# Seven block products in all fourteen inner tiles of a conv-GLU, with sums and a low part made by adding transfers

## The chip, the core and the metric

The kernel runs on one core of a Trainium2 chip. Its time is device microseconds of one execution of the program; the number compared is the median over runs. The engines are named as in the profile: PE multiplies matrices, PEld is its loading of weights, DVE (VectorE) and ACT (ScalarE) work element by element, POOL (GpSimd) and SP (SyncE) here issue transfers. Every engine takes its instructions in order, and they meet through semaphores.

## The reference, cut to what matters

The program computes two layers of an encoder trunk over 512 frames of width 1024: a time-mixing layer and a chunk-attention layer, each followed by the channel mixer that the change concerns. With D_FF = 2816:

```
def conv_glu(h, w_in, conv_w, conv_b, w_out):
    gate, val = jnp.split(h @ w_in, 2, axis=-1)             # (512, 1024) @ (1024, 2 * 2816)
    gp = jnp.pad(gate, ((0, 0), (2, 0), (0, 0)))
    conv = conv_b + sum(conv_w[j] * gp[:, j:j + 512] for j in range(3))
    return (jax.nn.gelu(conv) * val) @ w_out

x = x + conv_glu(rms_norm(x, ln2[layer]), ffn_in[layer], ffn_conv[layer], ffn_conv_b[layer], ffn_out[layer])
```

## The kernel before

All activations lie transposed, 128 channels on the partitions and 512 frames along a row. A product in full precision is made of three in the type float32r: a number is split into a high part (a rounding cast, on ACT) and a low part (what the rounding left, a subtraction on DVE), and high times high, high times low and low times high are summed in PSUM. `split_w` (lines 168 to 179) does it for weights: line 172 casts `whi`, and then either line 178 subtracts on DVE to give `wlo`, or, where a source in DRAM is given, line 175 writes the negated high part with ACT and line 176 lets POOL issue a transfer that adds the weights out of DRAM onto it. Before the change the second way is used in the first mixing layer and in part of an output projection alone. `wraw` has two buffers, `whi` and `wlo` have three each, handed out in turn to whoever splits weights next.

A channel mixer (`ffn`) makes 22 hidden tiles of 128 channels, j = 0 to 21, each from a gate tile and a value tile of weights (128 x 1024 floats, 512 KB each), and then an output stage. There are two kinds of hidden tile.

`eight(j)` multiplies plainly: for the gate and for the value 8 blocks of weights, three matmuls of 512 columns each, 48 matmuls in all (lines 201, 202 and 206, in `dense`).

`seven(j)` treats the gate and the value weights as a 2 x 2 matrix of halves, against two halves of the frames, and gets along with seven block products instead of eight (`prod`, lines 416, 417 and 419; each has 12 matmuls of 256 columns: eight with `whi`, alternating over the high and the low part of the activations, then four with `wlo`). Four of the products use sums of the activations that are made once per mixer (`sums`, tiles `xh` and parts of `f3h`, `f3l`); the others use the activations as they are. On the side of the weights each tile needs four sums or differences of halves (512 columns each), and the splits of all operands: `wv` (the value weights as loaded), `w1`, `w2`, `wx` and `w4`. Lines 435 and 439 to 441 make the sums on DVE. PSUM tiles `b` and `c` take up several products one after the other, and are read out (lines 447, 451, 456, 457, 461, 463) between one and the next. `gated(j, ...)` then applies convolution, gelu and gate (lines 389 to 393) and splits the hidden tile (lines 218 and 219).

Before the change the tiles 4, 5, 7, 8, 10, 11, 13, 14, 16 and 17 are sevens: ten of 22 in each of the two mixers, in pairs with an eight between them. The list is `SEVEN`. The loop in `ffn` runs the first product of a tile, then the last two products of the tile before it, then the tile's own middle. What is written there is not quite the order on the engines: a scheduler puts the instructions of DVE, ACT, POOL and SP in an order of its own, within the dependences. PE keeps to the program. A tile buffer that is handed out again makes its new writer wait for the last reader of the old content; on SP and POOL, where transfers are issued in order, everything behind a waiting issue waits too.

Of the kernel before, what the change touches and what calls it, by code (L numbers as in the profile page):

```python
# [13 lines left out]
ALU = mybir.AluOpType  # L14
# [98 lines left out]
def trunk_kernel(ctx, tc, A, out):  # L113
    nc = tc.nc
    PE, V, SC, GP = nc.tensor, nc.vector, nc.scalar, nc.gpsimd
# [28 lines left out]
    def ps_d(shape=(P, S)):  # L144
        return banks["D"].tile(list(shape), F32, name="psd", tag="psd")
# [7 lines left out]
    def ps_f(shape=(P, S)):  # L153
        return banks["F"].tile(list(shape), F32, name="psf", tag="psf")
# [8 lines left out]
    def tmp(dt=F32, shape=(P, S)):  # L163
        return banks["tmp"].tile(list(shape), dt, name="tmp", tag="tmp")
# [4 lines left out]
    def split_w(raw, n, src=None):  # L169
        hi = wp.tile([P, 1024], F32R, name="whi", tag="whi")  # L170
        lo = wp.tile([P, 1024], F32R, name="wlo", tag="wlo")
        SC.copy(hi[:, :n], raw)  # L172
        if src is not None:

            SC.activation(lo[:, :n], raw, AF.Copy, scale=-1.0)
            GP.dma_start(lo[:, :n], src, accum_op=ALU.add)
        else:
            V.tensor_tensor(lo[:, :n], raw, hi[:, :n], op=ALU.subtract)  # L178
        return hi, lo
# [37 lines left out]
    def split_to(h_, l_, src):  # L217
        SC.copy(h_, src)
        V.tensor_tensor(l_, src, h_, op=ALU.subtract)  # L219
# [124 lines left out]
            V.tensor_tensor(xT[:, m], xT[:, m], ps[:], op=ALU.add)  # L344
            norm_tile(xT[:, m], m, gain, h_, l_)

    SEVEN = [j for j in range(4, 18) if j % 3 != 0]
    HT = (slice(0, 256), slice(256, 512))

    def ffn(l, hp, ih, il, h_, l_, xT, after, last=None):  # L350
# [8 lines left out]
        def low(k):  # L359
            return (f3h, f3l)[k // 2][:, 10 + 2 * (k % 2):12 + 2 * (k % 2)]  # L360

        def high(k):
            return xh[0][:, 2 * k:2 * k + 2]
# [3 lines left out]
        def B(r, c):  # L367
            return lambda k: (ih[:, 4 * r + k, HT[c]], il[:, 4 * r + k, HT[c]])

        def T(n):  # L370
            n -= 1
            return lambda k: (high(k)[:, n // 2, HT[n % 2]], low(k)[:, n // 2, HT[n % 2]])

        def sums(k):
            u, w = tmp(), tmp()
            for t_, q in ((u, k), (w, k + 4)):
                nc.sync.dma_start(t_[:], xd[q])
                SC.activation(t_[:], t_[:], AF.Copy, scale=Vc(f"ln2_{l}", q))
            t12, t34 = tmp(), tmp()
            V.tensor_tensor(t12[:, HT[0]], u[:, HT[1]], u[:, HT[0]], op=ALU.subtract)  # L380
            V.tensor_tensor(t34[:, HT[0]], w[:, HT[1]], u[:, HT[1]], op=ALU.subtract)
            V.tensor_tensor(t12[:, HT[1]], w[:, HT[1]], t12[:, HT[0]], op=ALU.subtract)
            V.tensor_tensor(t34[:, HT[1]], w[:, HT[0]], t12[:, HT[1]], op=ALU.subtract)
            for n, t_ in enumerate((t12, t34)):
                split_to(high(k)[:, n], low(k)[:, n], t_[:])

        def gated(j, g, v):
            c = tmp()
            SC.activation(c[:], g[:], AF.Identity, scale=Vc(f"cw2_{l}", j), bias=Vc(f"cb_{l}", j))  # L389
            V.scalar_tensor_tensor(c[:, 1:S], g[:, 0:S - 1], Vc(f"cw1_{l}", j), c[:, 1:S], op0=ALU.mult, op1=ALU.add)  # L390
            V.scalar_tensor_tensor(c[:, 2:S], g[:, 0:S - 2], Vc(f"cw0_{l}", j), c[:, 2:S], op0=ALU.mult, op1=ALU.add)
            SC.activation(c[:], c[:], AF.Gelu)
            V.tensor_tensor(c[:], v, c[:], op=ALU.mult)
            split_to(*hid(j), c[:])
# [16 lines left out]
        def prod(ps, w, o, a, start=True):  # L411
            wh, wl = w
            for k in range(4):
                ws = slice(o + k * P, o + k * P + P)
                ah, al = a(k)
                PE.matmul(ps, wh[:, ws], ah, start=start and k == 0, stop=False, skip_group_check=not start)  # L416
                PE.matmul(ps, wh[:, ws], al, start=False, stop=False, skip_group_check=not start)  # L417
            for k in range(4):
                PE.matmul(ps, wl[:, o + k * P:o + k * P + P], a(k)[0], start=False, stop=k == 3,  # L419
                          skip_group_check=not start)  # L420

        def own(name, n):
            return tuple(hp.tile([P, n], F32R, name=name + q, tag=name + q) for q in "hl")

        def split2(w, raw):
            split_to(w[0][:], w[1][:], raw)
            return w

        def seven(j):
            rv = wp.tile([P, 1024], F32, name="wraw", tag="wraw", bufs=2)  # L430
            rg = hp.tile([P, 1024], F32, name="rg", tag="rg", bufs=2)
            nc.sync.dma_start(rv[:], A["ffn_in"][l, j, 1])
            nc.sync.dma_start(rg[:], A["ffn_in"][l, j, 0])
            one, two = slice(0, 512), slice(512, 1024)
            V.tensor_tensor(rg[:, one], rg[:, one], rg[:, two], op=ALU.add)
            wv = split_w(rv[:], 1024)
            w1 = split2(own("w1", 512), rg[:, one])
            w2 = split2(own("w2", 512), rg[:, two])
            V.tensor_tensor(rg[:, one], rg[:, one], rv[:, one], op=ALU.subtract)
            V.tensor_tensor(rg[:, two], rg[:, two], rg[:, one], op=ALU.subtract)  # L440
            V.tensor_tensor(rv[:, two], rv[:, two], rg[:, one], op=ALU.subtract)
            wx = split_w(rg[:], 1024)
            w4 = split2(own("w4", 512), rv[:, two])
            b, c = ps_d((P, 256)), ps_f((P, 256))
            v, g = tmp(), tmp()
            prod(b[:], wv, 0, B(0, 0))
            SC.copy(v[:, HT[0]], b[:])
            yield
            prod(c[:], w1, 0, T(1))
            prod(b[:], wx, 0, T(2), False)  # L450
            SC.copy(v[:, HT[1]], b[:])
            a = ps_f((P, 256))
            prod(a[:], wv, 512, B(1, 0))
            V.tensor_tensor(v[:, HT[0]], a[:], v[:, HT[0]], op=ALU.add)
            prod(b[:], wx, 512, T(3), False)
            SC.copy(g[:, HT[1]], b[:])
            V.tensor_tensor(g[:, HT[1]], c[:], g[:, HT[1]], op=ALU.add)
            V.tensor_tensor(g[:, HT[1]], g[:, HT[1]], rho[:, HT[1]], op=ALU.mult)
            yield
            prod(b[:], w2, 0, T(4), False)  # L460
            V.tensor_tensor(g[:, HT[0]], b[:], rho[:, HT[0]], op=ALU.mult)  # L461
            prod(c[:], w4, 0, B(1, 1), False)
            V.tensor_tensor(v[:, HT[1]], c[:], v[:, HT[1]], op=ALU.add)
            gated(j, g, v[:])

# [4 lines left out]
        for j in range(NFF):  # L470
            t = (seven if j in SEVEN else eight)(j)
            next(t)
            if rest is not None:
                run(rest)
                rest = None
            if j in SEVEN:
                next(t)
# [3 lines left out]
            if j < 2:  # L481
                sums(2 * j)
                sums(2 * j + 1)
            if j == SEVEN[-1] + 1:
                xT = mid.tile([P, KD, S], F32, name="xT", tag="xT")
# [950 lines left out]
```

## Time and profile before

| | us |
|---|---|
| median of three runs (lowest, highest) | 1346.57 (1345.35, 1353.61) |
| the profiled execution's own time | 1345.86 |
| its span on the core, first to last instruction | 1343.3 |
| first mixer, hidden tiles j = 0 to 21 | about 393 to 627 |
| second mixer, hidden tiles | about 975 to 1208 |

The mean granted TensorE clock of the profiled execution is 0.992. The time outside the span is 2.6 us. The profile's page gives busy times per engine, the span in forty slices, the transfers, the chain of work that ended last, and groups of instructions by source line and tile; further views answer for stretches of time, single lines and single transfers. A line of the groups reads: source line, engine, operation, tile written <- tiles read, shape, count | busy us in total, mean ns of one | idle time of the engine before them and what ended it. A row of the timeline begins with the start and the length in us.

### The profile page before, as it was taken

How to read it: one execution, taken by the hardware profiler on the slowest of the kernel's cores; microseconds unless marked ns; L12 is line 12 of the kernel's file. 1: busy time of each engine (PE TensorE's matmuls, PEld its weight loads, DVE VectorE, ACT ScalarE, POOL GpSimd, SP SyncE). 2: the span in 40 equal slices, each digit the busy share in tenths (PEclk: the TensorE clock that was granted, in tenths of full speed). 3: DMA queues.
4: the chain of work that ended last, by engine and by line, in shares of the span. 5: the costliest groups of instructions: out<-in, count | busy, mean ns of one | idle time of the engine just before them, and what ended most of it. 6: DMA issues, size and time to landing. Idle time of an engine off the chain costs nothing.

```text
span 1343.3 us, 22826 instructions
## 1 busy us (share of the span) xinstructions
PE 1303.2 (97%) x8986; PEld 1094.5 (81%) x8986; DVE 932.8 (69%) x2004; ACT 676.7 (50%) x1169; POOL 38.6 (3%) x77
## 2 busy tenths in 40 slices
PE   7999999999999999999999999999999999999996
PEld 5787777777788999988888878786889999988885
DVE  8886888877478888874444675657688888853335
ACT  6555465555357555553222576657565555532321
POOL 0000000000010000010000000000100000100000
PEclk9998999999999999999999999999999999999998
DMA  6365545463354333252333322232543333433332
GB/s 213 92 181 119 104 100 117 101 160 84 95 185 144 96 109 95 79 172 73 92 111 102 118 86 95 94 111 72 188 152 103 99 95 95 146 101 87 100 86 77
DMA packets 69050, 152.14 MB, mean 113 GB/s; under 512 B 25424, under 2 KB 29776, under 8 KB 68944
## 3 DMA queue, kind: packets, MB, share of 16 engines
q1 hardware_dynamic: 63648, 132.34, 32.4%
q0 software_dynamic: 5296, 18.35, 5.8%
q8 instruction: 70, 1.15, 0.4%
q14 instruction: 36, 0.29, 0.1%
HBM read 139.66 MB, written 11.01 MB: 112 GB/s over the span
## 4 chain that ended last, share of the span: by engine, by line
PE 83%; DVE 10%; ACT 3%; DMA 2%; issue 1%; SPq 0%; DVEq 0%; ACTq 0%
PE psd L201 11%; PE psd L202 10%; PE psd L206 10%; PE psf L201 7%; PE psf L202 7%; PE psf L206 6%; PE psd L416 3%; PE psd L419 3%; PE psd L417 3%; PE psf L419 2%; PE psf L417 2%; PE psf L416 2%; DVE Xu L798 1%; PE pss L1251 1%; DVE Xs L800 1%
## 5 line engine op out<-in xcount | busy, mean ns | idle before, releaser
L172 ACT CAST whi<-wraw 128x1024 fp32r<-128x1024 f32 (+1 forms) x182 | 187.3, 1030 | 285.6 <-DMA wraw<-in_ffn_out_dram 140.3
L178 DVE TENSOR_TENSOR wlo<-wraw,whi 128x1024 fp32r<-128x1024 f32 (+1 forms) x163 | 194.8, 1195 | 152.6 <-PE psd L206 69.0
L201 PE MATMUL psd<-r1h,whi 128*128 128x512 f32 x318 | 127.5, 401 | 0.0
L202 PE MATMUL psd<-r1l,whi 128*128 128x512 f32 x318 | 125.5, 395 | 0.0
L202 PE MATMUL psd<-f3l,whi 128*128 128x512 f32 (+1 forms) x238 | 88.6, 377 | 0.0
L201 PE MATMUL psd<-f3h,whi 128*128 128x512 f32 (+1 forms) x238 | 88.6, 377 | 0.0
L206 PE MATMUL psd<-r1h,wlo 128*128 128x512 f32 x318 | 86.4, 404 | 0.0
L201 PE MATMUL psd<-r2h,whi 128*128 128x512 f32 (+1 forms) x200 | 76.9, 389 | 0.8 <-ACT r2h L1258 0.7
L202 PE MATMUL psd<-r2l,whi 128*128 128x512 f32 (+1 forms) x200 | 76.3, 384 | 0.8 <-DVE r2l L219 0.8
L201 PE MATMUL psf<-r1h,whi 128*128 128x512 f32 x192 | 75.0, 391 | 0.0
L201 PE MATMUL psf<-r2h,whi 128*128 128x512 f32 x192 | 75.0, 391 | 0.0
L202 PE MATMUL psf<-r2l,whi 128*128 128x512 f32 x192 | 74.9, 390 | 0.0
L202 PE MATMUL psf<-r1l,whi 128*128 128x512 f32 x192 | 74.9, 390 | 0.0
L201 PEld LDWEIGHTS psd<-r1h,whi 128*128 128x128 f32 x318 | 59.8, 188 | 13.3 <-issue 0.5
L206 PEld LDWEIGHTS psd<-r1h,wlo 128*128 128x128 f32 x318 | 58.9, 192 | 12.9 <-issue 1.1
L202 PEld LDWEIGHTS psd<-r1l,whi 128*128 128x128 f32 x318 | 59.8, 188 | 11.7 <-issue 0.3
L206 PE MATMUL psd<-f3h,wlo 128*128 128x512 f32 (+1 forms) x238 | 53.7, 377 | 0.0
L201 PEld LDWEIGHTS psd<-f3h,whi 128*128 128x128 f32 x238 | 44.8, 188 | 8.2
L202 PEld LDWEIGHTS psd<-f3l,whi 128*128 128x128 f32 x238 | 44.8, 188 | 8.2
L206 PE MATMUL psd<-r2h,wlo 128*128 128x512 f32 (+1 forms) x200 | 50.3, 386 | 0.0
L389 ACT ACTIVATE tmp<-tmp,vec 128x512 f32<-128x512 f32 x44 | 35.9, 816 | 27.3 <-DVE tmp L461 16.5
L206 PEld LDWEIGHTS psd<-f3h,wlo 128*128 128x128 f32 x238 | 42.9, 188 | 8.2
(457 smaller groups left out, 3254.3 us busy)
## 6 DMA issues: line engine op xcount, KB each, us to landing
wraw<-in_ffn_in_dram SPq DMA_DIRECT2D x68, 512.0 KB, 3.7
wraw<-in_ffn_out_dram SPq DMA_DIRECT2D x32, 448.0 KB, 3.3
wraw<-in_wA_dram SPq DMA_DIRECT2D x20, 512.0 KB, 3.9
rg<-in_ffn_in_dram SPq DMA_DIRECT2D x20, 512.0 KB, 4.1
wraw<-in_w_out_dram SPq DMA_DIRECT2D x16, 512.0 KB, 3.7
wraw<-in_ffn_out_dram SPq DMA_DIRECT2D x16, 512.0 KB, 4.6
wlo<-in_wA_dram POOLq DMA_DIRECT2D x15, 512.0 KB, 7.5
xd<-xT POOLq DMA_DIRECT2D x16, 256.0 KB, 2.6
```

The costliest lines, as they stand in the source:

```text
L172: SC.copy(hi[:, :n], raw)
L178: V.tensor_tensor(lo[:, :n], raw, hi[:, :n], op=ALU.subtract)
L201: PE.matmul(ps, wh[:, j * P:(j + 1) * P], ah, start=start and n == 0, stop=False)
L202: PE.matmul(ps, wh[:, j * P:(j + 1) * P], al, start=False, stop=False)
L206: PE.matmul(ps, wl[:, j * P:(j + 1) * P], act(k)[0], start=False, stop=stop and n == len(ks) - 1)
L389: SC.activation(c[:], g[:], AF.Identity, scale=Vc(f"cw2_{l}", j), bias=Vc(f"cb_{l}", j))
L416: PE.matmul(ps, wh[:, ws], ah, start=start and k == 0, stop=False, skip_group_check=not start)
L417: PE.matmul(ps, wh[:, ws], al, start=False, stop=False, skip_group_check=not start)
L419: PE.matmul(ps, wl[:, o + k * P:o + k * P + P], a(k)[0], start=False, stop=k == 3, skip_group_check=not start)
L798: V.tensor_tensor(uv, L1.rearrange("p i o -> p o i").to_broadcast([P, k, n]), X[:, 0:k, q:q + 1].to_broadcast([P, k, n]), op=ALU.mult)
L800: V.tensor_tensor(X[:, 0:k, q + 1:], X[:, 0:k, q + 1:], uv, op=ALU.add)
L1251: PE.matmul(pso[HS[hh], kt * P:], vS[i // 2][:, kt, (i % 2 * 2 + hh) * 64:(i % 2 * 2 + hh + 1) * 64], pts[hh][:, kt, kt * P:], start=kt == ...
```

## The change

`SEVEN` becomes all of 4 to 17, so fourteen tiles in a row in each mixer. The operands of a seven are no longer made by the tile itself but one tile ahead, in three steps: `fetch(j)` loads the gate weights into `rg` and the value weights into `rv` (a `wraw` buffer), lets a transfer issued by POOL add the second half of the gate weights onto the first half of `rg`, and splits `rv` into `wv`, whose low part is now made by ACT and an adding transfer; `sums_a(j)` splits `w1`, makes three differences and splits what is left in `rg`; `sums_b(j)` splits `rv`, which then holds two differences, into tiles `wxh` and `wxl` of its own. The two operands of 512 columns `w2` and `w4` are thereby merged into operands of 1024: `wy` takes the place of one half of `wx` and of `w2`, the new `wx` that of the other half and of `w4`. While tile j is multiplied, `fetch(j + 1)` and `sums_a(j + 1)` stand in the program. In the middle of a tile the order of the first two products is swapped, except in the first seven of the row.

```
-    SEVEN = [j for j in range(4, 18) if j % 3 != 0]
+    SEVEN = list(range(4, 18))
...
-        def seven(j):
+        one, two = slice(0, 512), slice(512, 1024)
+        R, O = {}, {}
+
+        def fetch(j):
             rv = wp.tile([P, 1024], F32, name="wraw", tag="wraw", bufs=2)
             rg = hp.tile([P, 1024], F32, name="rg", tag="rg", bufs=2)
+            nc.sync.dma_start(rg[:], A["ffn_in"][l, j, 0])
             nc.sync.dma_start(rv[:], A["ffn_in"][l, j, 1])
-            nc.sync.dma_start(rg[:], A["ffn_in"][l, j, 0])
-            one, two = slice(0, 512), slice(512, 1024)
-            V.tensor_tensor(rg[:, one], rg[:, one], rg[:, two], op=ALU.add)
-            wv = split_w(rv[:], 1024)
+            GP.dma_start(rg[:, one], A["ffn_in"][l, j, 0][:, two], accum_op=ALU.add)
+            R[j] = rv, rg
+            O[j] = [split_w(rv[:], 1024, A["ffn_in"][l, j, 1])]
+
+        def sums_a(j):
+            rv, rg = R[j]
             w1 = split2(own("w1", 512), rg[:, one])
-            w2 = split2(own("w2", 512), rg[:, two])
             V.tensor_tensor(rg[:, one], rg[:, one], rv[:, one], op=ALU.subtract)
-            V.tensor_tensor(rg[:, two], rg[:, two], rg[:, one], op=ALU.subtract)
+            O[j] += [w1, split_w(rg[:], 1024)]
+            V.tensor_tensor(rv[:, one], rg[:, two], rg[:, one], op=ALU.subtract)
             V.tensor_tensor(rv[:, two], rv[:, two], rg[:, one], op=ALU.subtract)
-            wx = split_w(rg[:], 1024)
-            w4 = split2(own("w4", 512), rv[:, two])
+
+        def sums_b(j):
+            O[j].append(split2(own("wx", 1024), R.pop(j)[0][:]))
+
+        def seven(j):
+            nxt = j + 1 if j + 1 in SEVEN else None
+            if j not in O:
+                fetch(j)
+                sums_a(j)
             b, c = ps_d((P, 256)), ps_f((P, 256))
             v, g = tmp(), tmp()
-            prod(b[:], wv, 0, B(0, 0))
+            prod(b[:], O[j][0], 0, B(0, 0))
             SC.copy(v[:, HT[0]], b[:])
             yield
-            prod(c[:], w1, 0, T(1))
-            prod(b[:], wx, 0, T(2), False)
+            sums_b(j)
+            if nxt:
+                fetch(nxt)
+            wv, w1, wy, wx = O.pop(j)
+            if j - 1 not in SEVEN:
+                prod(c[:], w1, 0, T(1))
+            prod(b[:], wy, 0, T(2), False)
             SC.copy(v[:, HT[1]], b[:])
+            if j - 1 in SEVEN:
+                prod(c[:], w1, 0, T(1))
             a = ps_f((P, 256))
             prod(a[:], wv, 512, B(1, 0))
             V.tensor_tensor(v[:, HT[0]], a[:], v[:, HT[0]], op=ALU.add)
-            prod(b[:], wx, 512, T(3), False)
+            if nxt:
+                sums_a(nxt)
+            prod(b[:], wx, 0, T(3), False)
...
-            prod(b[:], w2, 0, T(4), False)
+            prod(b[:], wy, 512, T(4), False)
...
-            prod(c[:], w4, 0, B(1, 1), False)
+            prod(c[:], wx, 512, B(1, 1), False)
```

So PE's products follow each other, in a tile j inside the row, like this: `wv` (first half) of j; `wy` (second half) and `wx` (second half) of j - 1; then of j `wy` (first half), `w1`, `wv` (second half) and `wx` (first half).

Two places show how the engines' own order moves. The first is ACT in the first mixer. Before, in a pair of sevens and the eight behind it (`wraw_6575` and `wraw_6581` are the eight's weights; numbers tell buffers apart):

```order
L447 COPY tmp_6472<-psd_6470 128x256
L218 CAST w2h_6455<-rg_6443 128x512
L389 ACTIVATE tmp_6513<-tmp_6374,vec_67 128x512
L218 CAST w4h_6466<-wraw_6442 128x512
L172 CAST whi_6462<-rg_6443 128x1024
L172 CAST whi_6577<-wraw_6575 128x1024
L218 CAST w1h_6690<-rg_6682 128x512
L392 ACTIVATE tmp_6513<-tmp_6513 128x512
L451 COPY tmp_6472<-psd_6470 128x256
```

After, one whole tile of the row: it begins with the read-out of the tile before it (`psd_6356`), `wraw_6541` holds the value weights of the tile ahead, and `rg_6412`, `wraw_6411` belong to the tile that PE is at (`psd_6486`):

```order
L478 COPY tmp_6359<-psd_6356 128x256
L172 CAST whi_6465<-rg_6412 128x1024
L460 COPY tmp_6488<-psd_6486 128x256
L172 CAST whi_6546<-wraw_6541 128x1024
L175 ACTIVATE wlo_6547<-wraw_6541 128x1024
L389 ACTIVATE tmp_6529<-tmp_6359,vec_67 128x512
L218 CAST wxh_6537<-wraw_6411 128x1024
L469 COPY tmp_6488<-psd_6486 128x256
L392 ACTIVATE tmp_6529<-tmp_6529 128x512
```

The cast and the negation of the next tile's value weights now stand ahead of the gate's first step (line 389) and of the split of `wx`; before, no line 175 stood here at all.

The second place is POOL's queue in the same mixer. Before, it holds there the eight stores of the residual and their way back, with nothing between:

```order
L176 DMA wlo_4615<-in_w_out_dram 128x1024
L176 DMA wlo_4663<-in_w_out_dram 128x1024
L176 DMA wlo_4708<-in_w_out_dram 128x1024
L467 DMA xd_4967<-xT_76 128x512 x8
L487 DMA xT_7019<-xd_4967 128x512 x8
```

After, inside the row of sevens, each tile has two adding transfers, that of the gate sum (line 437) one tile ahead of that of the low part (line 176):

```order
L176 DMA wlo_6287<-in_ffn_in_dram 128x1024
L437 DMA rg_6412<-in_ffn_in_dram 128x512
L176 DMA wlo_6417<-in_ffn_in_dram 128x1024
L437 DMA rg_6542<-in_ffn_in_dram 128x512
L176 DMA wlo_6547<-in_ffn_in_dram 128x1024
```

POOL issues them strictly in turn: each waits for what it adds onto, and holds up the next.

## The prediction

> **What bounds the kernel now.** First the page: the span, the busy engines, the chain that ended last.
>
> ```profile
> span 1343.3 us, 22826 instructions
> ...
> PE 1303.2 (97%) x8986; PEld 1094.5 (81%) x8986; DVE 932.8 (69%) x2004; ACT 676.7 (50%) x1169; POOL 38.6 (3%) x77
> ...
> PE 83%; DVE 10%; ACT 3%; DMA 2%; issue 1%; SPq 0%; DVEq 0%; ACTq 0%
> ```
>
> PE is at work in 97% of the span and carries 83% of the chain. Inside the mixers it is the bound alone. The chain over the first mixer shows it; each row is the last part of a value product (start, length, what), that of tile 2 at 424.90, of tile 3 at 435.78, of tile 18 at 592.20:
>
> ```profile
> 424.90 1.81 PE psf L206 x8
> ...
> 435.78 1.81 PE psf L206 x8
> ...
> 592.20 1.81 PE psf L206 x8
> ```
>
> An eight thus takes 435.78 - 424.90 = 10.88 us. From 435.78 to 592.20 lie 156.42 us: ten sevens and five eights. Ten sevens took 156.42 - 5 x 10.88 = 102.0, 10.20 each; the fourteen tiles that the change touches took 156.42 - 10.88 = 145.5 us in a mixer.
>
> What could a seven take at best? The timeline of one (start, length, engine, line, operation, tiles, shape):
>
> ```profile
> 499.96 0.28 PE L416 MATMUL psd<-r2h,whi 128*128 128x256 f32 x1
> ...
> 500.80 0.28 PE L417 MATMUL psd<-r2l,whi 128*128 128x256 f32 x1
> 500.92 0.64 PE L419 MATMUL psd<-r2h,wlo 128*128 128x256 f32 x4
> ...
> 508.60 0.28 PE L416 MATMUL psd<-xh,w2h 128*128 128x256 f32 x1
> ```
>
> Six products lie between the first and the last row: 8.64 / 6 = 1.44 us each, so 7 x 1.44 = 10.08 a tile with no wait. In a product the low weights are needed 500.92 - 499.96 = 0.96 after its start, its high weights are free again 500.80 + 0.28 - 499.96 = 1.12 after it. Then how busy the others are, over a pair of sevens with an eight, and over an eight alone near the end (us; PE, PEld, DVE, ACT, POOL busy, clock, DMA share, GB/s):
>
> ```profile
> 468.86:500.13 31.27, 31.27 (x219) 29.21 (x218) 27.36 (x43) 17.34 (x27) 0.00 (x0) 1.00 0.32 102
> 599.45:610.33 10.88, 10.88 (x50) 9.01 (x49) 5.67 (x7) 4.07 (x5) 0.00 (x0) 1.00 0.32 96
> ```
>
> PE never stops. A seven costs DVE (27.36 - 5.67) / 2 = 10.85 us and ACT (17.34 - 4.07) / 2 = 6.64. DVE's 10.85 is more than the 10.08 in which PE could be done: sevens in a row, made as before, would be bound by DVE. The eights between them give it time.
>
> **The change part by part.** *The list.* Four more sevens in each mixer, at most 10.88 - 10.08 = 0.80 us each, and 0.12 on the ten that are sevens already, since the step from eight to seven goes away but for one: at the floor a mixer's fourteen tiles take 14 x 10.08 + 0.2 for that step = 141.3, 4.2 less than now; 8.4 in both. More than that the change cannot win, since everything else of PE's work stays.
>
> *DVE and ACT.* Rows of what leaves DVE and comes to ACT:
>
> ```profile
> L435 DVE TENSOR_TENSOR rg<-rg 128x512 f32<-128x512 f32 x20 | 13.7, 684 | 1.1 <-DMA rg<-in_ffn_in_dram 1.1
> L178 DVE TENSOR_TENSOR wlo<-rg,whi 128x1024 fp32r<-128x1024 f32 x20 | 24.4, 1218 | 0.0
> L175 ACT ACTIVATE wlo<-wraw 128x1024 fp32r<-128x1024 f32 x19 | 20.1, 1058 | 10.6 <-PE psd L206 9.2 <-PE psl L206 1.1
> L172 ACT CAST whi<-wraw 128x1024 fp32r<-128x1024 f32 (+1 forms) x182 | 187.3, 1030 | 285.6 <-DMA wraw<-in_ffn_out_dram 140.3 <-PE psd L202 38.4 <-PE psf L202 25.0
> ```
>
> DVE: 10.85 - 0.68 - 1.22 = 8.95 of 10.08, still 89%, but no bound. ACT: 6.64 + 1.06 = 7.7. The merged operands save a little more; taken at nothing. Both loads fit; what decides is the order of the waits.
>
> *The low part of the value weights, the longest chain.* There are three `whi` and three `wlo` buffers, and a tile now uses two, so the buffer for `wv` of tile j + 1 is that of `wy` of tile j - 1, which PE reads last in the first product that it runs after `wv` (first half) of tile j. From there: 1.12 until the high buffer is free, a cast of 1.03, the negated part of 1.06, POOL's issue, the transfer's landing L, and then PE needs it. How POOL's issue and the landing go, two issues of the same kind earlier in the kernel show, ACT's row ahead and SP's plain load beside it, and after each the landing of that POOL issue (smallest, median, largest; of one they are equal). The last row is that of all nineteen:
>
> ```profile
> 130.65 1.06 ACT L175 ACTIVATE wlo<-wraw 128x1024 fp32r<-128x1024 f32 x1
> 131.74 0.35 SPq L183 DMA_DIRECT2D wraw<-in_wA_dram  x1
> 132.01 0.86 POOL L176 DMA_DIRECT2D wlo<-in_wA_dram  x1 [15.00 <-ACT wlo L175]
> DMA to landing us min/median/max: 8.0/8.0/8.0
> ...
> 281.22 0.87 POOL L176 DMA_DIRECT2D wlo<-in_w_out_dram  x1 [9.73 <-ACT wlo L175]
> 283.42 2.02 SPq L785 DMA_DIRECT2D Lr<-d  x4
> DMA to landing us min/median/max: 5.4/5.4/5.4
> ...
> DMA to landing us min/median/max: 5.4/7.9/8.8
> ```
>
> POOL issues 132.01 - (130.65 + 1.06) = 0.30 after ACT ends. So the transfer starts 1.12 + 1.03 + 1.06 + 0.30 = 3.5 after the start of that product. PE comes to the low part six products and 0.96 later, 6 x 1.44 + 0.96 = 9.6. The cover is 9.6 - 3.5 = 6.1 us. With L up to 6.1 nothing waits; above it each tile waits L - 6.1, since the chain closes on itself once in a tile: a tile takes 3.98 + L.
>
> L is 5.4 where no plain load of weights starts near it, and 8.0 where SP started one of 512 KB 0.3 us ahead. In the new loop the next such load, `rg` of tile j + 2, is issued when DVE has done the low part of `wy` of tile j. Counting from the start of tile j on PE, DVE comes to it after the read-out of the last product and the differences, four operations of up to 0.7 and one of 1.22, at about 3.5. The adding transfer starts at 1.44 + 3.5 = 4.9, 1.4 later than the load. The load is then most of the way, not beside it; and if PE waits, the transfer moves back by the wait and the load does not, so that they part. The other load, `rv` of j + 2, is issued at about 8.1 (next part) and meets its end. I take L as 6.0 to 6.6, near the free row, with 5.4 and 8.8 as ends.
>
> The Trainium skill, "DMA: Bandwidth & Descriptors", in its section on the anatomy of one DMA on GpSimd's path, fits such a transfer by 2.0 us plus its bytes over 436e3; 512 KB would land after 3.2 us, and then no tile would wait. The rows above (5.4 to 8.8) disagree, and I use them.
>
> *The value weights themselves.* `rv` of j + 2 uses the buffer that is freed by the low part of `wx` of tile j. Cycle: load, cast 1.03, negation 1.06, line 389, 390, 391, then that low part (1.22 as line 178 above). Rows of those, and landings of such loads now (line 432):
>
> ```profile
> L389 ACT ACTIVATE tmp<-tmp,vec 128x512 f32<-128x512 f32 x44 | 35.9, 816 | 27.3 <-DVE tmp L461 16.5 <-DVE tmp L408 10.8
> L390 DVE SCALAR_TENSOR_TENSOR tmp<-tmp,vec 128x511 f32<-128x511 f32 x44 | 32.8, 746 | 1.8 <-ACT tmp L389 1.8
> L391 DVE SCALAR_TENSOR_TENSOR tmp<-tmp,vec 128x510 f32<-128x510 f32 x44 | 32.8, 746 | 0.5
> ...
> DMA to landing us min/median/max: 3.2/4.4/5.6
> ```
>
> 1.03 + 1.06 + 0.82 + 0.75 + 0.75 + 1.22 = 5.6; with a landing of 4.4 that is 10.0, just under 10.08; with 5.6 it is 11.2. (From the start of a tile: the negation ends at 4.6, and 0.82 + 0.75 + 0.75 + 1.22 later, at 8.1, the buffer is free.) The steps from one engine to the next are left out of both chains, but for POOL's 0.30; they add tenths. Two chains stand within a few tenths of PE's own time, then, and a pure floor is not likely.
>
> *The gate sum* is issued some 4 us after `rg`'s load and is needed more than a tile later; taken at nothing. If that cover were gone it would wait like the low part. *POOL's queue*: the first two gate sums stand between the stores of the residual. The loads that they wait for, the fifth store, and the first reader of the stores:
>
> ```profile
> 370.73 0.84 SPq L433 DMA_DIRECT2D rg<-in_ffn_in_dram  x2
> 378.71 0.54 POOL L467 DMA_DIRECT2D xd<-xT  x1 [6.26 <-DVE xT L344]
> 400.76 0.86 SPq L377 DMA_DIRECT2D tmp<-xd  x2
> ```
>
> The loads land some 4 us after 370.73, the fifth store waits until 378.71 for DVE anyway: hidden, and 22 us of cover beyond that.
> *Transfers*: a tile moves 512 + 512 KB plainly and 768 KB adding, 1.84 MB in some 10.2 us; the adding queue took this:
>
> ```profile
> q0 software_dynamic: 5296, 18.35, 5.8%
> ```
>
> 5.8% of 1343 is 78 us for 18.35 MB, so 0.79 MB take 3.3 us of all engines; the plain ones take 0.32 of 10.4 (window above) = 3.3. Together two thirds: no bound, but enough to make landings late now and then.
>
> **Sum.** Taking a wait of 0.17 a tile (L about 6.3): 14 x 10.25 + 0.2 = 143.7 in a mixer against 145.5; 3.6 us less in two. The profiled execution's 1345.86 becomes 1342.3. It is 0.7 under the median of the runs, so by that 1343.0.
>
> **Rivals.** *Floor*: both chains hide; 8.4 less, 1338.2. For it: DVE and ACT loads under PE's, the free landing of 5.4. Against: the nineteen landings' median of 7.9. The skill's fit named above would give this time.
> *The adding transfer meets plain loads after all*, the rival on the other side: L at its median 7.9 makes a tile 11.9, a mixer 14 x 11.9 + 0.2 = 166.8, 21.3 more; 42.6 in two: 1389. It decides from L = 6.4 (10.38 a tile, equal to now), and is 1% slower (13.5 us, 6.7 a mixer, 10.86 a tile) from L = 6.9. For it: most rows; against: the order in which load and transfer start.
> *The value weights come late*: a landing of 5.0 makes a tile 10.6, +3.1 a mixer, 1352.8; of 5.6, 11.2 and 1370. For it: today's largest; against: today's median.
> That the change does not do what it says is excluded by the engines' order, which shows fourteen tiles with both adding transfers.
>
> **How the numbers follow.** Small waits, 10.15 to 10.5 a tile (1340 to 1350): 0.45. Floor: 0.20. Value weights late: 0.14, half of it over 1%. Transfer late by 6.9 or more: 0.18. Rest: 0.03, mostly fast. 1% is about what a measurement of this kernel can tell from no change. Faster by that, 13.5 us, is beyond the 8.4 that PE leaves: 0.02. Slower: 0.18 + 0.07 = 0.25. Same: 0.73. The range goes from just under the floor, 1337, to 1368, where the rival on the other side has L = 7.2 (tile 11.2); some 0.16 is left out, nearly all above. The likeliest case alone: 1340 to 1350.
>
> **What would show it.** In the row of sevens PE's tiles 10.1 to 10.5 us apart, and where they are more than 10.08 a wait of PE on `wlo` or, through ACT, on `wraw`. Landings of the transfers onto `wlo` at 5.4 to 6.6 if right, 7 and over if the rival is. DVE busy some 9 us a tile. Wrong I would be if PE waited in the middle of a tile, on `wxh`, `whi` from `rg` or a read-out, because ACT and DVE come late in an order that I reckoned in sums.

## The result and the profile after

The changed kernel takes 1366.76 us (median of 6 runs, 1360.57 to 1372.93) against 1345.27 us of the kernel before, run beside it (median of 6, 1341.72 to 1353.61): a ratio of 1.0152, 95% interval 1.011 to 1.0195. It is 21.5 us slower, where 3.6 us less than before were forecast. The time lies just inside the range of the prediction, but on the other side of no change.

The page of the changed kernel, from top to bottom: span, busy time of each engine, the queue of POOL's transfers, the chain that ended last by engine, and of the transfers the row of those that add onto `wlo` in the mixers (KB of one, median us to landing).

```profile
span 1368.0 us, 23666 instructions
...
PE 1306.8 (96%) x9274; PEld 1108.5 (81%) x9274; DVE 925.9 (68%) x2008; ACT 717.0 (52%) x1217; POOL 87.6 (6%) x133
...
q0 software_dynamic: 13360, 40.38, 15.7%
...
PE 59%; DVE 15%; DMA 13%; ACT 6%; issue 5%; POOL 0%; SPq 0%; DVEq 0%; ACTq 0%; POOLq 0%
...
wlo<-in_ffn_in_dram POOLq DMA_DIRECT2D x28, 512.0 KB, 5.6
```

PE's share of the chain fell from 83% to 59%, and what came in is DMA (2% to 13%) and DVE (10% to 15%); POOL's queue, which carries the adding transfers, takes 15.7% of the DMA engines' time instead of 5.8%. The page still shows PE 96% busy: a wait of a microsecond in each of 28 tiles is 2% of the span and hardly moves that figure. The list of waits shows it. Its columns are: who waited and for what, us in all, how often, the longest. First the kernel before, where no transfer makes `wlo` in the mixers; then the changed one:

```profile
ACT whi L172 <- DMA wraw<-in_ffn_in_dram: 22.9, 11, 2.9
```

```profile
ACT whi L172 <- DMA wraw<-in_ffn_in_dram: 37.0, 22, 3.2
PEld psd L419 <- DMA wlo<-in_ffn_in_dram: 21.8, 22, 4.3
PE psd L419 <- DMA wlo<-in_ffn_in_dram: 17.2, 20, 4.1
```

The time between tiles is read from ScalarE's copy of a tile's first block product (line 460), which each seven has once. The first row is of the third seven of the first mixer, the second of the last:

```profile
463.26 0.37 ACT L460 COPY tmp<-psd 128x256 f32<-128x256 f32 x1
...
583.93 0.36 ACT L460 COPY tmp<-psd 128x256 f32<-128x256 f32 x1
```

Eleven tiles lie between them: 120.67 / 11 = 10.97 us each, where the floor is 10.08 and the forecast 10.25. What sets this is in the chain of waits over the same mixer (start, length, what). Two turns of it, the second without its middle, are this:

```profile
501.37 1.15 DVE wxl L219
502.51 0.02 issue
502.53 6.03 DMA wraw<-in_ffn_in_dram
...
509.59 1.05 ACT wlo L175
510.64 0.72 ACT tmp L389
511.36 0.02 issue
511.38 0.76 DVE tmp L390
512.15 0.02 issue
512.17 0.75 DVE tmp L391
512.92 1.15 DVE wxl L219
514.07 0.02 issue
514.08 5.40 DMA wraw<-in_ffn_in_dram
...
525.01 5.93 DMA wraw<-in_ffn_in_dram
```

No row of PE is in it. The low part of `wx` frees a raw buffer, the next value weights are loaded into it, cast and negated, the gate's three steps follow, and then comes the next low part: the ring that the prediction had under "The value weights themselves", 514.08 - 502.53 = 11.55 us in this turn, 6.03 of it the load and 5.52 all the rest. The next turn is 525.01 - 514.08 = 10.93, that is 5.40 + 5.53. It is the same all along the row: from the fourth load of a mixer to its last, nineteen of the twenty turns of the two mixers are the landing of their own load plus 5.52 or 5.53 us. Nothing else adds to a turn, so the landing alone makes it long. The ten last loads of a mixer land in 5.53 us on average in the first and 5.66 in the second, which gives 11.05 and 11.18 us; the tiles are 10.97 and 11.16 us apart. The timeline of the same stretch shows what runs beside that load (start, length, engine, line, operation, and in brackets the idle time before it):

```profile
499.39 0.87 POOL L176 DMA_DIRECT2D wlo<-in_ffn_in_dram  x1 [8.79 <-ACT wlo L175]
500.84 0.87 POOL L437 DMA_DIRECT2D rg<-in_ffn_in_dram  x1 [0.58 <-DVE tmp L390]
502.53 0.33 SPq L436 DMA_DIRECT2D wraw<-in_ffn_in_dram  x1
508.64 1.05 ACT L172 CAST whi<-wraw 128x1024 fp32r<-128x1024 f32 x1 [2.04 <-DMA wraw<-in_ffn_in_dram]
```

Both adding transfers of the tile go out 3.1 and 1.7 us ahead of the load, so that it is in flight together with both. The line that fills `rv` (436), its landings (smallest, median, largest), 4.4 in the middle before the change. All 28 loads are in it, also the first three of each mixer, which go out before both transfers are in flight and land in 3.4 to 3.7 us:

```profile
DMA to landing us min/median/max: 3.4/5.3/6.7
```

And the line that adds onto `wlo` (176, all 47 of the kernel):

```profile
DMA to landing us min/median/max: 5.4/5.8/9.5
```

### The profile page after: what moved, and what is told of

It reads as the page before. It is cut to its first block, busy times and chain, and to the rows that moved or that the text cites. A ratio compares the mean times of both kernels' runs of the same rounds, so it can differ in the third digit from the quotient of the medians.

```text
span 1368.0 us, 23666 instructions
## 1 busy us (share of the span) xinstructions
PE 1306.8 (96%) x9274; PEld 1108.5 (81%) x9274; DVE 925.9 (68%) x2008; ACT 717.0 (52%) x1217; POOL 87.6 (6%) x133
## 3 DMA queue, kind: packets, MB, share of 16 engines
q0 software_dynamic: 13360, 40.38, 15.7%
## 4 chain that ended last, share of the span: by engine, by line
PE 59%; DVE 15%; DMA 13%; ACT 6%; issue 5%; POOL 0%; SPq 0%; DVEq 0%; ACTq 0%; POOLq 0%
PE psd L201 10%; PE psd L202 10%; PE psd L206 10%; DMA wraw<-in_ffn_in_dram 6%; DMA wlo<-in_ffn_in_dram 3%; PE psf L201 3%; PE psf L202 3%; PE psf L206 2%; DVE Xu L820 1%; DVE wxl L219 1%; ACT wlo L175 1%; DVE Xs L822 1%; PE pss L1273 1%; DVE wlo L178 1%; PE psl L201 1%
## 5 line engine op out<-in xcount | busy, mean ns | idle before, releaser
L172 ACT CAST whi<-wraw 128x1024 fp32r<-128x1024 f32 (+1 forms) x174 | 178.9, 1029 | 297.2 <-DMA wraw<-in_ffn_out_dram 120.1
L178 DVE TENSOR_TENSOR wlo<-wraw,whi 128x1024 fp32r<-128x1024 f32 (+1 forms) x127 | 150.8, 1188 | 145.5 <-PE psd L206 68.9
L202 PEld LDWEIGHTS psd<-r1l,whi 128*128 128x128 f32 x318 | 60.0, 189 | 11.7 <-issue 0.3
L390 DVE SCALAR_TENSOR_TENSOR tmp<-tmp,vec 128x511 f32<-128x511 f32 x44 | 33.0, 749 | 40.1 <-ACT tmp L389 40.0
L416 PE MATMUL psd<-xh,whi 128*128 128x256 f32 x224 | 56.9, 286 | 0.0
L175 ACT ACTIVATE wlo<-wraw 128x1024 fp32r<-128x1024 f32 x47 | 49.5, 1054 | 10.1 <-PE psd L206 8.8
L201 PE MATMUL psf<-r1h,whi 128*128 128x512 f32 x128 | 50.0, 391 | 0.0
L201 PE MATMUL psf<-r2h,whi 128*128 128x512 f32 x128 | 50.0, 391 | 0.0
L202 PE MATMUL psf<-r1l,whi 128*128 128x512 f32 x128 | 49.9, 389 | 0.0
```

The costliest lines, as they stand in the source:

```text
L201: PE.matmul(ps, wh[:, j * P:(j + 1) * P], ah, start=start and n == 0, stop=False)
L202: PE.matmul(ps, wh[:, j * P:(j + 1) * P], al, start=False, stop=False)
```

## Experiments

Three theories went into the first three runs. *Theory 1*: the ring through the raw buffer sets the tile, the load's landing plus some 5.5 us. *Theory 2*: it is the adding transfer onto `wlo`, for which PE is seen to wait. *Theory 3*: the loads land late because of the gate sum's adding transfer beside them.

All runs in one table. "Two mixers" is the sum, over both, of the time from the first seven's read-out to the last one's (thirteen steps each; the kernel before has eights between), from the rows shown above for the changed kernel. "Load" is the median landing of the value weights, of all 28 (before: 20). These two columns are of the profiled execution of each kernel, the time is the median of all its executions: the profiled execution of "no gate transfer" took 1346.26 us, that of the idle transfer 1352.67.

| kernel | two mixers, us | load, us | time, us | ratio to before (95%) |
|---|---|---|---|---|
| before | 264.4 | 4.4 | 1345.1 to 1345.3 | |
| changed | 286.2 | 5.3 | 1366.76 | 1.0152 (1.011 to 1.0195) |
| third raw buffer | 265.0 | 5.3 | 1346.9 | 1.0018 (0.9995 to 1.0042) |
| gate sum on DVE | 260.1 | 3.8 | 1338.3 | 0.9949 (0.9929 to 0.9969) |
| low part on DVE | 257.1 | 4.0 | 1336.86 | 0.9956 (0.9912 to 1.0) |
| before, longer list | 277.3 | 4.0 | 1355.86 | 1.0087 (1.0058 to 1.0115) |
| `wx` low part first | 286.5 | 5.8 | 1366.98 | 1.015 (1.0107 to 1.0193) |
| both on DVE | 270.6 | 3.5 | 1349.36 | 1.0034 (1.0014 to 1.0054) |
| gate sum on DVE, idle transfer | 272.9 | 5.0 | 1357.48 | 1.0077 (1.0054 to 1.01) |
| third buffer, low part on DVE | 256.3 | 4.1 | 1337.04 | 0.9943 (0.9911 to 0.9974) |
| half of the gate transfer | 266.6 | 4.5 | 1347.36 | 1.0012 (0.9995 to 1.0029) |
| no gate transfer | 258.2 | 3.8 | 1340.39 | 0.9963 (0.9945 to 0.9981) |
| low part on DVE, again | 256.7 | 4.1 | 1335.93 | 0.9932 (0.9913 to 0.9951) |

The two mixers account for most of the loss: 286.2 - 264.4 = 21.8 us of the 24.0 by which the two profiled executions differ (1369.81 and 1345.86).

**A third raw buffer.** Every third tile's value weights have a buffer of their own, and the load of value weights is issued ahead of the gate weights'. The room comes from a slot of the hidden tiles that is idle until then.

```diff
+            if (j - SEVEN[0]) % 3 == 2:
+                rv = hp.tile([P, 1024], F32, name="rv", tag="rv")
+            else:
                 rv = wp.tile([P, 1024], F32, name="wraw", tag="wraw", bufs=2)
...
+            nc.sync.dma_start(rv[:], A["ffn_in"][l, j, 1])
             nc.sync.dma_start(rg[:], A["ffn_in"][l, j, 0])
-            nc.sync.dma_start(rv[:], A["ffn_in"][l, j, 1])
...
-            w1 = split2(own("w1", 512), rg[:, one])
+            w1 = split2((f3h[:, 9], f3l[:, 9]), rg[:, one])
```

> The changed kernel with a third buffer for the raw value weights: every third seven tile has its own, so a load of value weights goes out a tile earlier than in the changed kernel, ahead of the gate weights' load; the first weights' operands move into a hidden tile's slot that is idle then. Nothing is computed otherwise. Theory 1 (the loop through the raw buffer, load 5.3 us + cast to low part 5.5 to 5.8 us, sets the 11.1 us of a tile): the load is out of the loop, the cast no longer waits for it, a tile takes 10.1 to 10.3 us, 28 tiles save 22 to 28 us, the kernel takes 1338 to 1345 us. Theory 2 (the adding transfer onto the low part of the value weights is itself what TensorE waits for): its issue still stands behind the negation of the tile, tiles stay near 11 us, 1362 to 1367 us. Theory 3 (loads land late because the gate weights' adding transfer runs beside them): as theory 1 or a little over, 1340 to 1350 us, with the load's landing still 5 us or more.

It took 1346.9 us, 20 us less than the changed kernel, just above what theory 1 gave and inside the 1340 to 1350 of theory 3, which had kept the late landing. Its loads land as late as in the changed kernel. The load's line (438):

```profile
who waited for it (us, times):
  DVE rg L447: 0.6, 1
...
DMA to landing us min/median/max: 3.3/5.3/9.2
```

But ScalarE no longer waits for them. Its list of waits has of PE on the adding transfer:

```profile
PEld psd L419 <- DMA wlo<-in_ffn_in_dram: 8.0, 6, 3.5
PE psd L419 <- DMA wlo<-in_ffn_in_dram: 6.7, 4, 3.3
```

Twenty of the twenty-six steps between tiles are now 10.1 us. The adding transfer onto `wlo` is the same and lands no sooner (median 6.2 of 47, after 5.8), and yet PE's wait for it falls from 17.2 to 6.7 us. That speaks against theory 2: PE waited for `wlo` since its work began late, behind the late load. What is left over the floor is in the first step of the first mixer (9.4 us, where five products of 1.44 us make 7.2) and five steps of 10.3 to 11.5 us.

**The gate sum on DVE.** The one adding transfer is replaced by the sum that the kernel before had.

```diff
-            GP.dma_start(rg[:, one], A["ffn_in"][l, j, 0][:, two], accum_op=ALU.add)
+            V.tensor_tensor(rg[:, one], rg[:, one], rg[:, two], op=ALU.add)
```

> The changed kernel with the sum of the gate weights' halves made on VectorE (128x512, three operands in fp32) in place of the adding transfer. Theory 1: the load of the value weights stays in the loop, but is no longer beside that transfer; if it lands in 4.4 us as before the change, the loop is 10.0 to 10.3 us and the tile 10.2 to 10.5 us: 1341 to 1350 us; if it lands in 5 us or more all the same, because the adding transfer onto the low part runs beside it, 10.9 to 11.2 us and 1362 to 1367 us. Theory 2: as the changed kernel, 1364 to 1368 us. Theory 3 (the gate sum's transfer is what delays the load): 4.4 us, and 1341 to 1350 us.

It took 1338.3 us, under the ranges of all three theories. Theory 2 was farthest off, 26 us: the transfer onto `wlo` is as before, and by itself it costs little. The value weights' line (436), who waits for it and its landing:

```profile
  ACT whi L172: 4.3, 4
...
DMA to landing us min/median/max: 3.4/3.8/5.7
```

With 3.8 the ring is 3.8 + 5.5 = 9.3, under PE's 10.08, and drops out. Where a single load still comes late, it shows: one lands in 5.67 us, and that turn is 11.19.

**The low part of the value weights on DVE.** The other adding transfer goes, the gate sum's stays.

```diff
-            O[j] = [split_w(rv[:], 1024, A["ffn_in"][l, j, 1])]
+            O[j] = [split_w(rv[:], 1024)]
```

> The changed kernel with the low part of the value weights made on VectorE (128x1024) as before the change, in place of ScalarE's negation and the adding transfer; the gate sum stays an adding transfer. VectorE's work per tile goes from 8.95 us to about 10.1 us. Theory 1: the loop loses the negation (1.06 us) and gets the low part (about 1.2 us) ahead of the other sums on VectorE instead, so it stays at 10.8 to 11.3 us: 1360 to 1370 us, with TensorE's wait now through the last operand and no wait on a transfer. Theory 2 (the wait on the low part's landing sets the tile): that wait is gone, tiles 10.2 to 10.5 us, 1341 to 1350 us. Theory 3: the gate sum's transfer still runs beside the load, 1360 us or more.

1336.86 us: theory 1 by itself said 1360 or more and missed, since it kept the late landing, which was 4.0 here. So did theory 3, which blamed the gate sum's transfer alone. Theory 2 said 1341 or more and came nearest, but the run before had already gone against it. One transfer by itself hardly delays the load (3.8 and 4.0 us, against 3.5 with neither, below); both together do (5.3, so 1.8 us, where 0.3 and 0.5 make 0.8). Why it is more than the sum stays open; the gate sum's transfer also goes out longer ahead of the load in the changed kernel (1.7 us in the turn shown) than here, where it is mostly within half a microsecond of it. Between 440 and 560 us PE is busy all the time and DVE nearly so (us; PE, PEld, DVE, ACT, POOL busy, clock, DMA share, GB/s):

```profile
440.00:560.00 120.00, 120.00 (x1001) 119.93 (x1000) 116.89 (x186) 75.40 (x117) 9.51 (x11) 1.00 0.48 124
```

**The kernel before with the longer list.** Of the change only the list is made.

```diff
-    SEVEN = [j for j in range(4, 18) if j % 3 != 0]
+    SEVEN = list(range(4, 18))
```

> The kernel before with all of tiles 4 to 17 by seven block products and nothing else changed. The prediction said that sevens in a row made that way would be bound by VectorE at 10.85 us a tile: 14 tiles 151.9 us against the 145.5 us measured for the mix of sevens and eights, so about 6 us more in a mixer and 1355 to 1362 us. Against it: if the work ahead of the products, and not VectorE's sum, sets the tile there too, 11 us or more a tile and 1364 us or more; if TensorE's own 10.1 to 10.2 us a tile sets it, 1338 to 1342 us.

1355.86 us, as the prediction's remark on DVE would have it. Late in the first mixer the steps are 11.1 us, and DVE is at work in 63.82 of 65 us (columns as above); the chain of waits there goes through PE, ScalarE and DVE in turn, so that it is not DVE's sum alone:

```profile
510.00:575.00 65.00, 63.48 (x495) 60.27 (x494) 63.82 (x108) 38.82 (x64) 0.00 (x0) 1.00 0.25 89
```

**The low part of `wx` first.** It goes ahead of the second tap of the convolution on DVE, to make the ring 0.75 us shorter.

```diff
-            sums_b(j)
+            with tc.high_priority(offset=200):
+                sums_b(j)
```

> The changed kernel with the low part of the last operand (the one that frees the raw value weights) put ahead of the convolution's second tap on VectorE; both adding transfers stay. Theory 1 (loop through the raw buffer = landing + casts and sums up to that low part): the loop loses 0.75 us, the tile goes from 11.1 to 10.3-10.5 us if the load still lands in 5.3 us, 28 tiles save 17 to 22 us: 1345 to 1352 us. If the loop isn't what sets the tile (TensorE waits on the adding transfer as such), 1362 us or more.

1366.98 us: nothing won. The load now lands in 5.8 instead of 5.3 us. One turn of the ring in the timeline (start, length, engine, line, operation, in brackets the idle time before it):

```profile
509.42 0.33 SPq L436 DMA_DIRECT2D wraw<-in_ffn_in_dram  x1
...
515.97 1.05 ACT L172 CAST whi<-wraw 128x1024 fp32r<-128x1024 f32 x1 [2.24 <-DMA wraw<-in_ffn_in_dram]
516.92 1.05 ACT L175 ACTIVATE wlo<-wraw 128x1024 fp32r<-128x1024 f32 x1
517.88 0.80 ACT L389 ACTIVATE tmp<-tmp,vec 128x512 f32<-128x512 f32 x1
...
518.72 0.75 DVE L390 SCALAR_TENSOR_TENSOR tmp<-tmp,vec 128x511 f32<-128x511 f32 x1 [2.47 <-ACT tmp L389]
519.39 0.42 DVE L486 TENSOR_TENSOR tmp<-psf,tmp 128x256 f32<-128x256 f32 x1
519.72 1.21 DVE L219 TENSOR_TENSOR wxl<-wraw,wxh 128x1024 fp32r<-128x1024 f32 x1
520.96 0.33 SPq L436 DMA_DIRECT2D wraw<-in_ffn_in_dram  x1
```

The ring is closed as before, without a gap: load, cast, negation, line 389 and 390, low part, next load. It did get shorter, though by 0.45 us and not by 0.75, because another operation of DVE (line 486) slipped in ahead of the low part: in seventeen of the twenty turns the landing plus 5.06 or 5.07 us is the whole turn, in place of 5.52. But the landings of the ten last loads of a mixer grew from 5.53 and 5.66 to 5.93 and 6.20 us on average, and that takes back all of it. So theory 1 was right about what sets the tile, and wrong in holding the landing fixed. The load goes out 2.7 us behind the transfer onto `wlo` here (520.96, and 518.27 for that transfer) instead of 3.1, which may be why it lands later; this was not tried by itself. The profile's chain of waits for this kernel goes another way through the same stretch, over the transfer onto `wlo` and PE; the rows above leave nothing for that way to set.

**Both on DVE.** Both edits above together: no adding transfer is left, and of the change stay the list, the merged operands and the preparing one tile ahead.

> The changed kernel with neither adding transfer: gate sum and low part of the value weights both on VectorE, all else (list of tiles, preparing one tile ahead) as changed. Theory 1 with 3: no transfer disturbs the load (4 us), but VectorE has 8.95 + 0.68 + 1.22 = 10.85 us a tile to do, so tiles of 10.9 to 11.1 us and 1351 to 1358 us, near the kernel before with the longer list (1355.9). If VectorE's sum does not set the tile and the work ahead does, 10.1 to 10.3 us and 1335 to 1340 us.

1349.36 us, 1.6 us under the lower end of the range for a bound by DVE. The load lands in 3.5 us. After a first step of 7.2 us the next seven steps are 9.7 to 10.6 us, and then they are 11.4 us, with DVE at work 52.28 of 55 us. DVE is nearly as busy in the first stretch, so it seems to fall behind there and to live on what was prepared ahead; that is read from these rows and not shown by a run of its own:

```profile
440.00:500.00 60.00, 60.00 (x501) 59.91 (x500) 57.62 (x93) 36.45 (x58) 0.00 (x0) 1.00 0.29 96
520.00:575.00 55.00, 53.54 (x412) 50.22 (x412) 52.28 (x84) 31.21 (x48) 0.00 (x0) 1.00 0.26 85
```

Against the longer list alone that is 6.5 us less. With the two kernels that keep one transfer it gives the account of the change, from no adding transfer: either one alone saves 11 to 13 us (1338.3 and 1335.93 against 1349.36), since it takes 0.68 or 1.22 us a tile off DVE; the two together cost 17 (1366.76).

**An idle transfer beside the gate sum on DVE.** An adding transfer of 256 KB, out of the loaded gate weights into an idle slot that nothing reads, at the place of the one taken away.

```diff
+            if j == 4:
+                GP.dma_start(f3h[:, 9].bitcast(F32), rg[:, two])
+            elif j < 17:
+                GP.dma_start(f3h[:, 9].bitcast(F32), rg[:, two], accum_op=ALU.add)
```

> The kernel with the gate sum on VectorE, and at the place of the taken-away adding transfer an adding transfer of the same size (256 KB, on-chip source) into an idle slot, which nothing reads. It differs from the kernel with the gate sum on VectorE by that transfer alone. If two adding transfers in flight are what delays the load of the value weights, it lands in 5 us or more again and the tile is 10.8 to 11.2 us: 1358 to 1368 us. If what hurt was that the gate sum's result was waited for, it lands in 3.8 us and the time stays at 1338 us.

1357.48 us, 19 more than without it and 0.5 under the range forecast. The value weights' line, who waits for it and its landing:

```profile
  ACT whi L172: 22.8, 18
...
DMA to landing us min/median/max: 3.5/5.0/6.5
```

No engine waits for the result of this transfer but POOL with its next one (8.4 us, in two places), and the turns of the ring are again the landing plus 5.52 us, so the loss comes from its being in flight. It reads on-chip memory, where the changed kernel's reads the weights from outside, which may be why the landing is 5.0 and not 5.3.

**Half of the gate transfer, and none.** In the changed kernel it moves 128 KB, or nothing; the gate sum is left out for half of the columns, or for all. The edit shown is that of half; for none the line is left out.

```diff
-            GP.dma_start(rg[:, one], A["ffn_in"][l, j, 0][:, two], accum_op=ALU.add)
+            GP.dma_start(rg[:, 0:256], A["ffn_in"][l, j, 0][:, 512:768], accum_op=ALU.add)
```

> The changed kernel with the gate weights' adding transfer cut to half of its columns (128 KB instead of 256 KB); the rest of the gate sum is left out. Nothing else is moved. If the bytes of the adding transfers beside the load of the value weights delay it, the landing comes between 3.8 us (no such transfer) and 5.3 us, about 4.5 us, the loop is 10.1 to 10.4 us and the kernel takes 1340 to 1352 us. If it is the number of transfers and not their size, the landing stays at 5 us or more and the time at 1360 us or more.

> The changed kernel without the gate weights' adding transfer and with nothing in its place (the gate sum is left out). It differs from the changed kernel by that transfer alone. Landing of the value weights 3.8 us as with the sum on VectorE, tiles of 10.1 us, 1335 to 1339 us: then all that the change lost, and the 28 tiles' 21 us beside it, is the price of this one transfer. If the time stays over 1350 us, the other adding transfer loses it by itself.

1347.36 us with half, 1340.39 with none (1.4 us over the range), 1366.76 with all. The value weights' line with half:

```profile
  ACT whi L172: 10.4, 12
...
DMA to landing us min/median/max: 3.4/4.5/5.9
```

So the landing goes 3.8, 4.5, 5.3 us for 0, 128 and 256 KB: 1.5 us for 256 KB. An estimate from the two pages agrees: POOL's queue moves 40.38 - 18.35 = 22.03 MB more in the changed kernel, all of it adding, and takes 137 us more of all engines (15.7% of 1368.0 against 5.8% of 1343.3), 6.2 us a MB, which is 1.6 us for 256 KB. The two mixers go 258.2, 266.6, 286.2 us: the first half costs 8.4 us, the second 19.6, as a ring does that reaches PE's time only on the way (4.5 + 5.5 = 10.0, just under 10.08). The Trainium skill, "DMA: Bandwidth & Descriptors", section Queues, rings and completion order, says that a DMA engine takes turns between the rings it has work for, a packet at a time; a landing that grows with the other ring's bytes agrees with that. No run here shows the turns themselves.

**Third buffer and low part on DVE; low part on DVE once more.** Whether the two remedies add up, and the fastest kernel again for a narrower interval.

> The changed kernel with the third raw buffer and the low part of the value weights on VectorE (the gate sum stays an adding transfer). Theory 1: either alone took the loop below TensorE's 10.1 us a tile, so both together give nothing more: 1335 to 1342 us, with tiles at 10.1 us. If the tiles with the third buffer alone still lost time to the landing, 1333 to 1336 us.

> The kernel with the low part of the value weights on VectorE once more, for a narrower interval: 1335 to 1339 us, 0.5 to 0.7 % under the kernel before (TensorE's own 10.08 us a tile for 14 tiles instead of 145.5 us saves 4.4 us a mixer, 8.8 us together).

1337.04 and 1335.93 us: they don't add up, since one alone takes PE to its floor. The kernel with the low part on DVE is faster than both kernels of this case: 0.9932 of the kernel before (0.9913 to 0.9951), 9.2 us.

## Why the prediction was wrong

**The step that failed** is the size of one term: under "The value weights themselves" the landing of the load was taken at 4.4 us, the median of the kernel before, where nothing adds beside it. It measured 5.3 in the middle of all loads, and 5.53 and 5.66 on average in the ring of the two mixers. The ring itself was as the prediction had it, and the rest of that sum held: cast to low part was put at 5.6 and takes 5.52. With the measured landings it gives 11.05 and 11.18 us, against steps of 10.97 and 11.16. The text had this case as a rival, 10.6 us a tile and 1352.8 for a landing of 5.0, 11.2 and 1370 for 5.6, and the result lies between. It had 0.14, on the argument "today's median". That argument used a row in which the new cause is absent, although the paragraph on transfers, further on, reckoned DMA at two thirds and landings late "now and then". The share was right, 0.67 measured from 440 to 585 us. Its parts were not: the 18.35 MB that it took for adding transfers hold 8.4 MB of plain stores and their way back, and by the 6.2 us a MB of the estimate above the adding of a tile takes 4.9 us of all engines and not 3.3. Nor was "now and then": line 436 is issued in each tile at the same place, just behind both adding transfers (1.7 and 3.1 us in the turn shown), so that half of its landings are 5.3 us or more, and not a few.

**The coupling of the two chains** was missed too, and with it the forecast's own 0.17 us of waiting a tile was put on the wrong chain. The prediction let the low part's chain start with the buffer that PE frees, with a cover of 6.1 us. Its landing, 5.6 us in the mixers, was even under the 6.0 to 6.6 taken, and by that sum PE would not have waited at all. It waited 17.2 us, since the cast came only with the late load (2.04 us of waiting in the turn shown). Two chains that begin with the same load are one case, not two that hide each other.

**The big rival on the other side**, an adding transfer delayed by plain loads to 7.9 us, did not come: the transfer onto `wlo` went out 3.1 us ahead of the load and landed in 5.6 us. The delay fell on the plain load and on the other adding transfer, that of the gate sum, which lands in 6.8 us in the middle, 4.0 at least.

**The gate sum "taken at nothing"** was right for its result, for which ScalarE waits 7.7 us in one place, and wrong for its bytes: without the transfer the kernel takes 1340.39 us, 26 us less. The prediction asked who waits for a transfer, and not what the transfer is in the way of.

**What held.** PE's floor: most steps at 10.1 us wherever one of the two transfers or the ring was taken away, and 9.2 us won where 8.4 was the sum (by the interval 6.6 to 11.7). DVE's 10.85 us as a bound for sevens in a row: 11.1 us measured with the longer list, 11.4 late in the kernel with both sums on DVE. POOL's issue, 0.30 us behind ScalarE: 0.30 again (510.94 after 509.59 + 1.05). The estimate of 3.2 us for 512 KB by the fit of the Trainium skill, "DMA: Bandwidth & Descriptors", section Anatomy of one DMA (GpSimd's path), stays under every landing onto `wlo` here: they take 5.3 us at least in any of these kernels.

## What to carry to other kernels

Work that is moved from an engine to a transfer is not free when nobody waits for it: look at what else is in flight at the time of its issue, and take the landing of those loads with it, not from the profile before. Where a load refills a buffer that is freed late in each turn of a loop, add up the ring (landing, and all that stands in order up to the freeing); if it is within a microsecond of the bound, a small delay of the load is the loop's time. Do not hold the landing fixed when the ring is made shorter either: here a ring shorter by 0.45 us met loads that landed that much later. Of two such moves, do one: here each of them wins 0.5 to 0.7%, and both lose 1.5%.

## What was not expected of the hardware

The bytes in flight decided when a plain load landed: one of 512 KB lands in 3.8 us behind an adding transfer of 512 KB, in 4.5 with 128 KB of adding more, in 5.3 with 256 KB more, while the adding transfer onto `wlo`, which goes out about 3 us ahead of it, lands in 5.6 to 5.7 us in all of these (median of the 28 in the mixers). And a loop can run near its floor for eight tiles and slow down only then (steps of 9.7 to 10.6 us, then 11.4, with both sums on DVE).
